# New durations in a kernel's emission-order model, a 128-row up-projection and a weight stream of its own

## The chip, the core and the metric

The kernel runs on one core of one Trainium2 chip. The metric is the device time of one execution in microseconds. The kernel of before took 1872.74 us, the median of three runs (1870.92, 1872.74 and 1876.2).

## What is computed

One step of an encoder layer: RMS norm, one input projection for two groups of heads, a mixer in each group, a SiLU gate, one output projection, and a second norm with a residual. There are T = 1088 tokens: a prompt of 1024 and a sample of 64 that continues a cache of 128. Cut to what matters:

```python
h = _rms_norm(x, norm_pre, NORM_EPS)
proj = h @ w_in                                    # 1024 -> 8320 columns
# group A: 8 heads of differential attention, two softmaxes per head
q, k = _partial_rope(...), _partial_rope(...)
s = jnp.einsum('bqhcd,bkhcd->bchqk', q, k).astype(F32) * (A_QK_DIM ** -0.5)
s = jnp.where(visible[None, None, None], s, -jnp.inf)
p = jax.nn.softmax(s, axis=-1)
wgt = p[:, 0] - lam * p[:, 1]
o = jnp.einsum('bhqk,bkhd->bqhd', wgt.astype(v.dtype), v)
y_a = _rms_norm(o, subln, SUBLN_EPS) * (1.0 - lambda_init) * silu(gate_a)
# group B: 16 heads of RWKV-7 with a 64 x 64 state each
w_log = -softplus(-(w0 + jnp.tanh(wd) @ w_up)) - 0.5        # wd, ad: 64 columns
a = jax.nn.sigmoid(a0 + ad @ a_up)
s = s * w_t + sa * b_t + v_t * k_t                 # per token, sa = s @ a_t
y_b = (group_norm(s @ r_t) + bonus) * silu(gate_b)
out = concat(y_a, y_b) @ w_out                     # 2048 -> 1024
x_new = x + _rms_norm(out, norm_post, NORM_EPS)
```

## The kernel before, in words

**The four kinds of work.** (1) The input projections: `proj_cm` (L208) makes 128 columns of `proj` for all tokens, as three chunks of 384, 384 and 320 tokens; each chunk is 8 times 3 matmuls, since every operand is split into a high and a low half (L215 high x high, L216 high x low, L217 low x high). (2) Group B: `unit` (L476) handles one pair of heads over 512 tokens; there are 16 of them, and one more for the sample that holds all 16 heads (17 in all). A unit takes the up-projection of decay and rate (L513 with the high half of the weights, L514 with the low half), elementwise work, the inverse of a triangular matrix in levels (L684 and L694), and then a serial chain over eight steps of 64 tokens. A step of the chain is three times the same alternation of TensorE (PE) and VectorE (DVE): L804 makes `g` and DVE copies it (L818), L821 makes `uu` and DVE copies it into `suv` (L827 and L828), L832 makes the state's update and DVE adds it (L842). The unit ends with a norm, transposes (L906) and its output to DRAM. Its matmuls L804 to L833 go through one PSUM bank, `cbank`. (3) Group A, `phase_a`: per head `prep` loads and splits queries and keys, `score` makes the scores of a tile of 128 queries (L1322 and L1323), reduces their maximum on DVE (L1332) and takes the exponential on ScalarE (ACT, L1348); `qtile` combines the two softmaxes on DVE (L1370), transposes the weights (L1381), copies them out (L1385 on DVE, L1389 on ACT), multiplies by the values (L1395), and ends with a norm and a gate (L1412 and after). Heads run one after the other. (4) The output projection, `out_projection` (L1041): 72 `jobs`, which are 8 groups of contraction rows and output columns by 9 tiles of tokens. Groups 0 to 3 need only group B's output, groups 4 and 5 the first four heads of A, group 6 heads 4 and 5, group 7 heads 6 and 7. A job is 12 matmuls of 512 columns (L1145, L1146 and L1147) in L1145's loop, and its result is added up in SBUF by ACT or DVE. The weights of a group are loaded by `load_wo` (L1074; 8 DMAs of 256 columns, each followed by a split on ACT and POOL), the tokens' side by `load_mix` (L1090); `loader` (L1108) goes over the jobs and starts both.

**What sets the order.** All instructions are emitted by one scheduler, the class `Weave` (L64). Every piece of work above is a stream (a Python generator) with a rank: the units have 0 to 16 and come first, the projections of group A follow as filling with rank 100, the heads of A have ten ranks each, the output projection fills at rank 99. `Weave` holds a model time `now`. A stream emits some instructions, says what they cost (`spend(ns)` for PE, `op(engine, n)` for an operation of n elements on another engine, which returns the time until its result is there), and yields for so long. At every turn the stream of lowest rank whose time has come goes on; if none is due, model time jumps. So the durations of the model say how much filling is put between a matmul and the one that needs its result by way of DVE or ACT. The framework then places semaphores and moves some instructions within an engine's queue, so the order that results is read from the built program. The lines that set the model are

```python
LA, LAT, W_LD, W_DMA = 130, 100, 11000, 3122                   # L42
...
    def spend(self, ns):
        self.now += ns
    def op(self, eng, n):
        self.free[eng] = max(self.now, self.free.get(eng, 0.0)) + RS * (RATE[eng] * n + 80)
        return self.free[eng] - self.now + (LA if b_done[0] else LAT)
```

DMAs of both `load_wo` and `load_mix` are issued by the queue of SyncE (SP), and so are most of the heads' loads and the outputs.

Of the kernel before, what the change touches and what calls it, by code (L numbers as in the profile page):

```python
# [21 lines left out]
P = 128  # L22
# [19 lines left out]
LA, LAT, W_LD, W_DMA = 130, 100, 11000, 3122  # L42
# [4 lines left out]
RS = 1.0  # L47
RATE = {DVE: 1 / 0.96, ACT: 1 / 1.2, POOL: 2.4}

# [9 lines left out]
class Weave:  # L59
# [7 lines left out]
    def __init__(self):  # L67
        self.now = 0.0
        self.live = []
        self.free = {}  # L70
        self.count = itertools.count()
# [46 lines left out]
def layer(ctx: ExitStack, tc: tile.TileContext, I, O):  # L118
# [105 lines left out]
    def raw_rows(tag):  # L224

        raw = rp.tile([P, T + 1], F32, tag="raw", bufs=2, name=f"raw_{tag}")
        nc.gpsimd.memset(raw[:, 0:1], 0.0)

        def evac(ps, t0, n):
            nc.scalar.copy(raw[:, 1 + t0:1 + t0 + n], ps)  # L230
        return raw, evac
# [50 lines left out]
def phase_b(tc, I, O, E):  # L282
# [8 lines left out]
    with ExitStack() as bs:  # L291
# [68 lines left out]
        def shift(raw, idx, dest):  # L360
# [34 lines left out]
        def pair_job(nm, p, w):  # L395
# [10 lines left out]
            if nm == "g":  # L406
                h0, h1 = yield from tiles()

                def evac(ps, t0, n):
                    for s0, s1, d in ((0, HALF, h0), (HALF, TP, h1), (TP, T, gs_[:, p, :])):  # L410
# [5 lines left out]
                        stt(d_, d_, 1.0, ps[:, a - t0:b - t0], op0=ADD, op1=MUL)  # L416
                yield from proj_cm(w, evac, f"g{p}")
# [58 lines left out]
        def unit(n, p, hf):  # L476
# [21 lines left out]
            for q0 in range(0, 8, 4) if smp else (0,):  # L498
# [43 lines left out]
            spend(1100)  # L542
# [13 lines left out]
            yield op_(DVE, 512)  # L556
# [62 lines left out]
            op_(POOL, 960)  # L619
            op_(ACT, 512)  # L620
# [6 lines left out]
            for g in range(2):  # L627
# [7 lines left out]
                spend(1800)  # L635
# [9 lines left out]
                yield done(op_(DVE, 6 * 256 + 400), 2)  # L645
# [26 lines left out]
            d = op_(DVE, 800)  # L672
# [7 lines left out]
            for lv in range(1, 6):  # L680
# [4 lines left out]
                spend(300)  # L685
# [9 lines left out]
                spend(500)  # L695
# [15 lines left out]
            spend(500)  # L711
# [12 lines left out]
            spend(600)  # L724
# [7 lines left out]
            for h in range(2):  # L732
# [5 lines left out]
                spend(500)  # L738
# [27 lines left out]
            spend(500)  # L766
# [35 lines left out]
            for c in range(8):  # L802
# [41 lines left out]
                op_(DVE, 110)  # L844
                if c % 4 == 3:
# [7 lines left out]
                    op_(ACT, 400)  # L853
                    op_(ACT, 400)
                yield op_(DVE, 110)
# [8 lines left out]
            yield op_(DVE, 1200)  # L864
# [9 lines left out]
            yield op_(POOL, 700)  # L874
# [3 lines left out]
            z_at = weave.now + op_(POOL, 110)  # L878
# [45 lines left out]
            vtt(yo, yo, gate, op=MUL)  # L924
            if smp:
# [6 lines left out]
        def fill_job(kind, h, w):  # L932
# [3 lines left out]
            def evac(ps, t0, n):  # L936
                if kind == "g":
                    act(st_[:, t0:t0 + n], ps, AF.Tanh, scale=0.5)
                    stt(st_[:, t0:t0 + n], st_[:, t0:t0 + n], 1.0, ps, op0=ADD, op1=MUL)  # L939
                else:  # L940

                    act(st_[:, t0:t0 + n], ps, AF.Copy, scale=0.125 if kind == "q" else 1.0)
            yield from proj_cm(w, evac, f"a{kind}{h}")
# [9 lines left out]
        def rope(kd, g):  # L953
            W = T // 8
            for j in range(8):
# [10 lines left out]
                vtt(a, a, b, op=ADD)  # L966
                nc.sync.dma_start(out=E["rots"][kd, g, 2][:, cl], in_=a)
# [72 lines left out]
def out_projection(tc, I, O, E):  # L1040
# [95 lines left out]
    weave.add(99, loader())  # L1136
    for i, (g, tt) in enumerate(jobs):
# [26 lines left out]
def phase_a(tc, I, O, E):  # L1164
# [49 lines left out]
    def prep(h):  # L1214
# [75 lines left out]
        for c in range(2):  # L1290
# [5 lines left out]
            spend(450)  # L1296
# [9 lines left out]
    def score(i, h, qt, c, st):  # L1306
# [12 lines left out]
        for o_, w in parts:  # L1319
# [4 lines left out]
            spend(w / 1.2 + 20)  # L1324
        yield LA
        nb = ap_.tile([P, 3], F32, tag=f"nb{c}", bufs=3, name=f"nb{u}")
        for i_, (s, (o_, w)) in enumerate(zip(ss, parts)):
            if qt < 8 and i_ == m - 1:

                nc.vector.memset(s[0:64, w - 64:w], -(2.0 ** 100))  # L1330
                op_(DVE, 60)
# [3 lines left out]
        if m > 1:  # L1335
            mx = nb[:, 2:3]
            vtt(mx, nb[:, 0:1], nb[:, 1:2], op=ALU.min)  # L1337
            d = op_(DVE, 60)
# [158 lines left out]
```

## Time and profile before

| what | value |
|---|---|
| runs of before | 1876.2, 1870.92, 1872.74 us; median 1872.74 |
| the profiled execution | 1870.95 us, of which the span of its instructions is 1869.1 us |
| granted TensorE clock, mean over the span | 0.975 of full speed |
| PE, busy share of the span | 91% (12,930 matmuls) |
| DVE / ACT / POOL, busy share | 70% / 46% / 37% |
| DMA | 158.85 MB, mean 85 GB/s |

The profile is of one execution. A busy share is a mean over the span; the span has stages with different limits: group B's units come first, then group A's attention with the output projection, then the last jobs and the final norm. An instruction's line is that of the kernel of before; in the kernel of after the same instructions stand 12 to 20 lines further down (L513 and L514 at L526 and L527, L215 to L217 at L224 to L226, L804 at L818, L821 at L835, L832 at L846, L906 at L919, L1145 to L1147 at L1165 to L1167, L1322 and L1323 at L1342 and L1343, L1381 at L1401, L1395 at L1415).

### The profile page before, as it was taken

The page shows a single profiled execution, that of the slowest core. Times are in us where ns is not written, and L with a number is a line of the kernel's source. Part 1 is how long each engine was busy: PE and PEld are TensorE (multiplying, and loading weights), DVE is VectorE, ACT ScalarE, POOL GpSimd, SP SyncE. Part 2 cuts the span into 40 slices and gives each one's busy share as a digit, 9 for nine tenths or more (in the row PEclk, how much of TensorE's full clock was granted, in tenths as well). Part 3 has the DMA queues.
Part 4 walks back from the last instruction along what each step waited for, and adds up shares of the span by engine and source line. Part 5 has one row for each costly group of instructions (what it writes and reads, how often), then busy time and mean ns, then how long its engine had stood idle before and what let it go on. Part 6 is the DMA issues. An engine that isn't in the chain of part 4 may idle for free. (4 is left out here: it accounts for less than half of the span.)

```text
span 1869.1 us, 34871 instructions
## 1 busy us (share of the span) xinstructions
PE 1699.6 (91%) x12930; PEld 1500.6 (80%) x12930; DVE 1305.8 (70%) x2892; ACT 868.1 (46%) x2155; POOL 695.4 (37%) x866
## 2 busy tenths in 40 slices
PE   6999899999998999999999899977899798889995
PEld 5888888888888888888888789877778676777784
DVE  5568777777778787886875766524687667787336
ACT  5534444344344444444443433323566576676323
POOL 4442333233233323323332421212332356554657
PEclk9999999999999999999999999998999899899998
DMA  4110111321122111110101121345555565443325
GB/s 144 49 55 27 50 48 48 80 82 36 39 72 62 51 44 35 52 38 29 57 26 50 57 62 50 106 118 160 153 156 149 165 155 156 121 131 105 116 87 181
DMA packets 204244, 158.85 MB, mean 85 GB/s; under 512 B 44229, under 2 KB 185194, under 8 KB 204074
## 3 DMA queue, kind: packets, MB, share of 16 engines
q1 hardware_dynamic: 169242, 137.33, 25.5%
q10 hardware_dynamic: 34832, 19.30, 4.0%
q8 instruction: 102, 1.67, 0.4%
q14 instruction: 68, 0.56, 0.1%
HBM read 108.67 MB, written 47.34 MB: 83 GB/s over the span
## 5 line engine op out<-in xcount | busy, mean ns | idle before, releaser
L1348 ACT ACTIVATE e<-s,nb 128x512 f32<-128x512 f32 (+4 forms) x208 | 117.3, 569 | 59.3 <-DVE nb L1332 26.1
L1145 PE MATMUL po<-woh,mxh 128*128 128x512 f32 x288 | 120.3, 419 | 7.1 <-DVE part L1156 5.9
L1147 PE MATMUL po<-wol,mxh 128*128 128x512 f32 x288 | 115.9, 402 | 3.9 <-DVE nb L1337 2.5
L1146 PE MATMUL po<-woh,mxl 128*128 128x512 f32 x288 | 115.5, 401 | 4.2 <-POOL mxl L158 4.2
L1332 DVE TENSOR_REDUCE nb<-s 128x1 f32<-128x512 f32 (+4 forms) x208 | 108.0, 529 | 15.9 <-PE s L1323 14.6
L158 POOL TENSOR_TENSOR mxl<-mxr,mxh 128x512 fp32r<-128x512 f32 (+1 forms) x72 | 88.3, 1231 | 74.9 <-ACT mxh L157 61.8
L811 ACT ACTIVATE sd<-suv,dc 64x64 f32<-64x64 f32 x128 | 44.4, 347 | 154.1 <-DVE suv L842 149.4
L1322 PE MATMUL s<-k,qs 128*128 128x512 f32 (+4 forms) x208 | 78.9, 385 | 22.0 <-ACT k L1249 10.0
L1395 PE MATMUL x_o<-vn,wt 128*128 128x128 f32 (+1 forms) x608 | 88.0, 289 | 10.1 <-DVE wt L1385 5.4
L1395 PEld LDWEIGHTS x_o<-vn,wt 128*128 128x128 f32 (+1 forms) x608 | 81.0, 200 | 18.5 <-issue 5.5
L1156 DVE TENSOR_TENSOR part<-po,part 128x512 f32<-128x512 f32 x72 | 49.5, 688 | 55.6 <-PE po L1147 55.5
L842 DVE SCALAR_TENSOR_TENSOR suv<-cbank,dc,sd 64x64 f32<-64x64 f32 x224 | 63.0, 281 | 33.3 <-PE cbank L832 29.2
L832 PE MATMUL cbank<-suv,bkt 128*128 128x128 f32 x256 | 56.9, 304 | 32.0 <-DVE suv L828 32.0
L832 PEld LDWEIGHTS cbank<-suv,bkt 128*128 128x128 f32 x256 | 41.1, 190 | 45.7 <-DVE suv L828 43.4
L215 PE MATMUL pj_v<-hhi,wh_v 128*128 128x384 f32 (+1 forms) x192 | 70.1, 365 | 6.5 <-DVE mg L416 6.1
L1409 POOL TENSOR_SCALAR ms<-ms 128x1 f32<-128x1 f32 x72 | 18.0, 249 | 150.9 <-ACT osq L1407 150.4
L1323 PE MATMUL s<-k,qs 128*128 128x512 f32 (+4 forms) x208 | 71.5, 358 | 2.4 <-POOL k L1252 1.5
L215 PE MATMUL pj_av<-hhi,wh_av 128*128 128x384 f32 (+1 forms) x192 | 70.2, 365 | 3.0 <-DVE fl_g L939 3.0
L157 ACT CAST mxh<-mxr 128x512 fp32r<-128x512 f32 (+1 forms) x72 | 40.7, 567 | 68.7 <-PE po L1147 29.4
L677 POOL TENSOR_TENSOR ltlo<-lt,lt 64x512 f16<-64x512 f32 x32 | 37.7, 1177 | 93.4 <-ACT lt L665 92.2
L1145 PEld LDWEIGHTS po<-woh,mxh 128*128 128x128 f32 x288 | 55.4, 192 | 20.6 <-DVE part L1156 4.4
L215 PE MATMUL pj_k<-hhi,wh_k 128*128 128x384 f32 (+1 forms) x192 | 67.7, 352 | 4.0 <-ACT raw_k L230 4.0
(533 smaller groups left out, 6189.5 us busy)
## 6 DMA issues: line engine op xcount, KB each, us to landing
mxr<-mixB SPq DMA_DIRECT2D x32, 256.0 KB
wor<-in_w_out SPq DMA_DIRECT2D x64, 128.0 KB
qa<-scr_q SPq DMA_DIRECT2D x32, 204.0 KB
ka<-scr_k SPq DMA_DIRECT2D x32, 204.0 KB
scr_q<-fl_q SPq DMA_DIRECT2D x8, 544.0 KB
scr_k<-fl_k SPq DMA_DIRECT2D x8, 544.0 KB
scr_v<-fl_v SPq DMA_DIRECT2D x8, 544.0 KB
scr_g<-fl_g SPq DMA_DIRECT2D x8, 544.0 KB
```

Of the source, the lines that this page charges most:

```text
L158: gtt(lo, raw, hi.bitcast(F32), op=SUB)
L215: mm(ps[:, :n], hi[:, k, :], hhi[i][:, k, :], start=(k == 0), stop=False)
L832: mm(s, bkt[:, c], suv[:, c], start=True, stop=True)
L842: stt(suv[r, c + 1, h, :] if c < 7 and not smp else to[r], s[r, h * CH:(h + 1) * CH], dc[r, c:c + 1], sd[r], op0=MUL, op1=ADD)
L1145: mm(ps, hi[:, q, :], wh, start=(q == 0), stop=False)
L1146: mm(ps, lo[:, q, :], wh, start=False, stop=False)
L1147: mm(ps, hi[:, q, :], wl, start=False, stop=(q == len(ks) - 1))
L1322: mm(s[:, 0:w], lq, k1[c][:, k0 + o_:k0 + o_ + w], start=True, stop=False)
L1323: mm(s[:, 0:w], lq, k2[c][:, k0 + o_:k0 + o_ + w], start=False, stop=True)
L1332: nc.vector.tensor_reduce(nb[:, i_:i_ + 1], s[:, 0:w], axis=AX.X, op=MAX, negate=True)
L1348: act(e[:, o_:o_ + w], s[:, 0:w], AF.Exp, bias=mx, accum_out=sm)
L1395: mm(ops[:, 0:P], wt[0:w, b, :], vn[0:w, vb, :], start=(b == 0), stop=(b == len(kbs) - 1))
```

## The change

Three things change. First, the model's durations: fixed costs per operation (`FIX`), a latency of 210 ns after matmuls and 60 ns after other engines in place of 130 and 100, a cost for switching to and from matmuls that use only part of the 128 rows (`T_IN`, `T_OUT`), new numbers in many calls of `spend` and `op_`, and calls for operations that the model did not have. Second, the low half of the up-projection (L514) multiplies all 128 rows of `t` and `x`, where it took the 64 rows that hold the high half of `x`; so it also adds low x low. Third, the weights of the output projection are loaded by a stream of their own (`w_loader`, rank 99.2), group after group, each as soon as the group before the last is done; before, `loader` started that when it came to a group's first job, behind its waits for the tokens' side. The core of the diff:

```diff
-LA, LAT, W_LD, W_DMA = 130, 100, 11000, 3122
+LAT, OUT, W_LD, W_DMA = 210, 60, 11000, 3122
+LA = LAT
+
+T_IN, T_OUT = 130, 105
...
+FIX = {DVE: 150, ACT: 190, POOL: 90}
...
-    def spend(self, ns):
+    def spend(self, ns, part=False):
+
+        if part != self.part:
+            self.part = part
+            ns += T_IN if part else T_OUT
         self.now += ns
 
-    def op(self, eng, n):
-
-        self.free[eng] = max(self.now, self.free.get(eng, 0.0)) + RS * (RATE[eng] * n + 80)
-        return self.free[eng] - self.now + (LA if b_done[0] else LAT)
+    def op(self, eng, n, k=1, at=0.0):
+
+
+        self.free[eng] = max(self.now + at, self.free.get(eng, 0.0)) + RATE[eng] * n + k * FIX[eng]
+        return self.free[eng] - self.now + OUT
...
                 for q, t in enumerate(ups):
-                    for j, (x, r) in enumerate(((xw, slice(0, 64)), (xa, slice(64, 128)))):
+                    for j, x in enumerate((xw, xa)):
...
                         mm(o_, t[:, j], x[:, cl], start=True, stop=False)
-                        mm(o_, t[r, 2 + j], x[r, cl], start=False, stop=True)
+                        mm(o_, t[:, 2 + j], x[:, cl], start=False, stop=True)
                 spend(900)
...
-                spend(500)
+                spend(340, True)
                 yield LAT
                 xn = t512("xt", 2, F16, nm=f"{lv}{u}")
...
-            spend(w / 1.2 + 20)
+            spend(w / 1.1 + 10)
         yield LA
...
-        op_(ACT, n)
-        return op_(POOL, n)
+        return op_(POOL, n, at=op_(ACT, n))
...
     def loader():
         for q, (g, tt) in enumerate(jobs):
-            if q % 9 == 0:
-                yield lambda: done[0] >= 9 * (g - 1)
-                weave.add(99.2, load_wo(g))
             yield lambda: there(g, tt) and q < done[0] + MB and len(mix) + done[0] >= q - 1
             weave.add(99.1, load_mix(q))
             yield 10
+
+    def w_loader():
+
+        for g in range(8):
+            yield lambda: done[0] >= 9 * (g - 1)
+            yield from load_wo(g)
...
     weave.add(99, loader())
+    weave.add(99.2, w_loader())
```

How this moves instructions on PE is read from the built programs, at three places. In the rows a name ends in a running number of the allocation, and "x2" is a run of two.

**First place: the up-projection of the first unit of head pair 3.** `m_up` is the up-projection, `xw` and `xa` its inputs, `t_wus` the weights, `pj_` a chunk of a projection, `y` and `cbank` belong to the chain of the unit before. Before:

```order
L694 MATMUL m_iq12_10_5076<-xt_a2_1_4974,q16_12_1_5037 64x64
L804 MATMUL cbank_509<-suv2_0_4717,pt0_498 128x128
L809 MATMUL y2_00_4807<-suv2_0_4717,pt0_498 128x128
L513 MATMUL m_up3_00_5068<-xw_466,t_wus3_00_5070 128x512
L514 MATMUL m_up3_00_5068<-xw_466,t_wus3_00_5070 128x512
L513 MATMUL m_up3_01_5069<-xa_467,t_wus3_00_5070 128x512
L514 MATMUL m_up3_01_5069<-xa_467,t_wus3_00_5070 128x512
L215 MATMUL pj_r3_0_5062<-hhi0_173,wh_r3_4843 128x384
```

and of the change:

```order
L225 MATMUL pj_av0_0_5348<-hlo0_176,wh_av0_5092 128x384
L226 MATMUL pj_av0_0_5348<-hhi0_173,wl_av0_5093 128x384
L224 MATMUL pj_av0_0_5348<-hhi0_173,wh_av0_5092 128x384
L225 MATMUL pj_av0_0_5348<-hlo0_176,wh_av0_5092 128x384
L226 MATMUL pj_av0_0_5348<-hhi0_173,wl_av0_5093 128x384
L526 MATMUL m_up3_00_5379<-xw_466,t_wus3_00_5381 128x512
L527 MATMUL m_up3_00_5379<-xw_466,t_wus3_00_5381 128x512
L526 MATMUL m_up3_01_5380<-xa_467,t_wus3_00_5381 128x512
L527 MATMUL m_up3_01_5380<-xa_467,t_wus3_00_5381 128x512
```

The four matmuls stand together in both; the projections around them (`pj_r3`, a chunk of this unit's own inputs, before; `pj_av0`, a chunk of group A's, after) are others.

**Second place: a step of the chain of the last unit, 7_1.** `gsb` and `suv` are what DVE hands over between L821 and L832 (L835 and L846), `po` are the output projection's results. Before:

```order
L215 MATMUL pj_ak5_2_14946<-hhi2_175,wh_ak5_14536 128x320
L216 MATMUL pj_ak5_2_14946<-hlo2_178,wh_ak5_14536 128x320
L217 MATMUL pj_ak5_2_14946<-hhi2_175,wl_ak5_14537 128x320
L821 MATMUL cbank_509<-gsb7_14_14958,xtf_504 128x128
L824 MATMUL y7_14_14954<-suv7_1_14687,pt0_498 128x128
L215 MATMUL pj_ak5_2_14946<-hhi2_175,wh_ak5_14536 128x320
L216 MATMUL pj_ak5_2_14946<-hlo2_178,wh_ak5_14536 128x320
L217 MATMUL pj_ak5_2_14946<-hhi2_175,wl_ak5_14537 128x320
L215 MATMUL pj_ak5_2_14946<-hhi2_175,wh_ak5_14536 128x320
L216 MATMUL pj_ak5_2_14946<-hlo2_178,wh_ak5_14536 128x320
L217 MATMUL pj_ak5_2_14946<-hhi2_175,wl_ak5_14537 128x320
L832 MATMUL cbank_509<-suv7_1_14687,bkt7_1_14656 128x128
```

and of the change:

```order
L1166 MATMUL po000_16272<-woh90_16234,mxl00_16219 128x512
L1167 MATMUL po000_16272<-wol90_16235,mxh00_16218 128x512
L818 MATMUL cbank_509<-suv7_1_15879,pt0_498 128x128
L838 MATMUL y7_14_16034<-suv7_1_15879,pt0_498 128x128
L1165 MATMUL po010_16288<-woh90_16234,mxh01_16224 128x512
L1166 MATMUL po010_16288<-woh90_16234,mxl01_16225 128x512
L835 MATMUL cbank_509<-gsb7_14_16038,xtf_504 128x128
L1165 MATMUL po000_16272<-woh100_16248,mxh00_16218 128x512
L1166 MATMUL po000_16272<-woh100_16248,mxl00_16219 128x512
L1167 MATMUL po000_16272<-wol100_16249,mxh00_16218 128x512
L846 MATMUL cbank_509<-suv7_1_15879,bkt7_1_15848 128x128
L847 MATMUL y7_14_16034<-suv7_1_15879,rbk7_1_15188 128x128
```

Before, projections of head 5 stand between the chain's matmuls, six of them between L824 and L832; after it all projections are used up and the output projection's matmuls stand there, three in that gap.

**Third place: head 3, tile 5.** `s3_5` are scores, `x_wt` transposed weights, `x_o` the product with the values. Before:

```order
L1381 MATMUL x_wt3_20_18161<-ident_79,e3_20_18091 128x128 x2
L1322 MATMUL s3_41512_18154<-k131_17847,qs31_17822 128x128
L1323 MATMUL s3_41512_18154<-k231_17865,qs31_17822 128x128
L1145 MATMUL po000_18238<-woh80_17903,mxh00_17909 128x512
L1395 MATMUL x_o3_8_18184<-vn3_17377,wt3_8_18099 128x128 x2
L1146 MATMUL po000_18238<-woh80_17903,mxl00_17910 128x512
L1322 MATMUL s3_500_18190<-k130_17800,qs30_17760 128x512
L1323 MATMUL s3_500_18190<-k230_17820,qs30_17760 128x512
L1147 MATMUL po000_18238<-wol80_17904,mxh00_17909 128x512
L1145 MATMUL po010_18318<-woh80_17903,mxh01_17915 128x512
L1381 MATMUL x_wt3_30_18200<-ident_79,e3_30_18133 128x128 x4
L1322 MATMUL s3_50512_18193<-k130_17800,qs30_17760 128x256
```

and of the change:

```order
L1343 MATMUL s3_410_19084<-k231_18842,qs31_18797 128x512
L1415 MATMUL x_o3_8_19068<-vn3_18328,wt3_8_19033 128x128 x2
L1342 MATMUL s3_41512_19087<-k131_18817,qs31_18797 128x128
L1343 MATMUL s3_41512_19087<-k231_18842,qs31_18797 128x128
L1401 MATMUL x_wt3_20_19094<-ident_79,e3_20_19039 128x128 x3
L1315 MATMUL x_kt31_19106<-ident_79,ka31_18321 128x64 x8
L1342 MATMUL s3_500_19130<-k130_18763,qs30_18744 128x512
L1343 MATMUL s3_500_19130<-k230_18795,qs30_18744 128x512
L1342 MATMUL s3_50512_19133<-k130_18763,qs30_18744 128x256
L1343 MATMUL s3_50512_19133<-k230_18795,qs30_18744 128x256
L1401 MATMUL x_wt3_30_19136<-ident_79,e3_30_19048 128x128 x4
L1415 MATMUL x_o3_2_19141<-vn3_18328,wt3_2_19093 128x128 x3
```

Before, output-projection matmuls stand one by one between the attention's; after it none is there, and the attention's matmuls follow each other.

## Rows read from the trace of the kernel before

**Rows 1.** The page's part 1: busy time and share of each engine.
```profile
PE 1699.6 (91%) x12930; PEld 1500.6 (80%) x12930; DVE 1305.8 (70%) x2892; ACT 868.1 (46%) x2155; POOL 695.4 (37%) x866
```

**Rows 2.** Stretches: length; busy of PE, PEld, DVE, ACT, POOL; clock, DMA share, GB/s.
```profile
100.00:1240.00 1140.00, 1079.45 (x9432) 973.92 (x9431) 840.02 (x1818) 471.98 (x1076) 352.28 (x419) 0.99 0.18 53
1300.00:1740.00 440.00, 391.92 (x2381) 333.76 (x2380) 326.05 (x842) 280.43 (x843) 197.38 (x254) 0.96 0.53 143
1821.00:1869.00 48.00, 29.18 (x110) 20.50 (x108) 31.83 (x37) 16.87 (x34) 34.65 (x44) 0.89 0.53 179
```

**Rows 3.** Timeline of PE at one up-projection: start us, duration us, instruction.
```profile
1076.23 0.40 PE L513 MATMUL m_up<-xw,t_wus 128*128 128x512 f32 x1
1076.56 0.50 PE L514 MATMUL m_up<-xw,t_wus 64*128 64x512 f32 x1
1076.99 0.50 PE L513 MATMUL m_up<-xa,t_wus 128*128 128x512 f32 x1
1077.42 0.49 PE L514 MATMUL m_up<-xa,t_wus 64*128 64x512 f32 x1
1077.85 0.49 PE L804 MATMUL cbank<-suv,pt 128*128 128x128 f32 x2
```

**Rows 4.** Timeline of PE: output projection, projection in a run, projection after another kind.
```profile
1764.80 0.39 PE L1145 MATMUL po<-woh,mxh 128*128 128x512 f32 x1
1765.03 0.39 PE L1146 MATMUL po<-woh,mxl 128*128 128x512 f32 x1
...
604.56 0.34 PE L215 MATMUL pj_v<-hhi,wh_v 128*128 128x384 f32 x1
604.73 0.34 PE L216 MATMUL pj_v<-hlo,wh_v 128*128 128x384 f32 x1
...
601.92 0.44 PE L215 MATMUL pj_v<-hhi,wh_v 128*128 128x384 f32 x1
602.20 0.34 PE L216 MATMUL pj_v<-hlo,wh_v 128*128 128x384 f32 x1
```

**Rows 5.** Timeline of PE in the sample unit's up-projection (L514 lies between).
```profile
1013.83 0.28 PE L513 MATMUL m_upNone<-xw,t_wusNone 128*128 128x64 f32 x1
...
1014.26 0.30 PE L513 MATMUL m_upNone<-xa,t_wusNone 128*128 128x64 f32 x1
```

**Rows 6.** Instructions of one line: ns min/median/max, first to last start us, forms.
```profile
L906 PE MATMUL m_zt<-ident,ycp x128: 270/272/327, 194.5 to 1233.0; 128*128 128x128 f32 x128
L1322 PE MATMUL s<-k,qs x208: 218/391/795, 1262.7 to 1726.1; 128*128 128x512 f32 x72, 128*128 128x128 f32 x8, 128*128 128x256 f32 x8, 128*128 128x192 f32 x8
L1395 PE MATMUL x_o<-vn,wt x608: 270/275/582, 1275.8 to 1738.7; 128*128 128x128 f32 x151, 64*128 64x128 f32 x1
```

**Rows 7.** PE's waits, 100 to 1240 us: total us, times, longest us.
```profile
PE cbank L832 <- DVE suv L828: 32.0, 36, 3.2
PE cbank L821 <- DVE gsb L818: 7.7, 9, 1.8
```

**Rows 8.** Tile cbank in the last unit, 1196 to 1223 us (two records a matmul).
```profile
L832 PE MATMUL cbank<-suv,bkt x14: 271/275/377, 1196.2 to 1222.5; 128*128 128x128 f32 x14
```

**Rows 9.** Stretches of the attention, columns as in rows 2.
```profile
1341.00:1682.50 341.50, 302.86 (x1840) 256.27 (x1840) 258.29 (x664) 225.96 (x671) 158.48 (x197) 0.97 0.55 148
...
1460.60:1471.40 10.80, 8.03 (x51) 5.76 (x49) 10.01 (x39) 6.02 (x22) 0.74 (x2) 1.00 0.67 200
1471.40:1477.00 5.60, 0.40 (x2) 0.20 (x2) 0.14 (x1) 1.72 (x5) 1.03 (x1) 0.58 0.93 318
1253.80:1274.30 20.50, 6.98 (x27) 5.86 (x27) 6.68 (x21) 8.28 (x18) 5.54 (x3) 0.50 0.77 198
...
1541.00:1552.00 11.00, 8.99 (x53) 6.69 (x52) 10.21 (x26) 8.05 (x28) 1.18 (x3) 1.00 0.62 175
```

**Rows 10.** Groups by line on DVE, 1341 to 1682.5 us.
```profile
L1332 DVE TENSOR_REDUCE nb<-s 128x1 f32<-128x512 f32 (+4 forms) x156 | 81.1, 529 | 13.3 <-PE s L1323 12.3
```

**Rows 11.** ACT's waits for mix loads, 1440 to 1740 us.
```profile
ACT mxh L157 <- DMA mxr<-mixB: 10.9, 4, 5.7
```

More of the change, by code (lines that the diff above doesn't have):

```diff
@@ L230, in evac @@
             nc.scalar.copy(raw[:, 1 + t0:1 + t0 + n], ps)
+            weave.op(ACT, n, at=LAT)
         return raw, evac
@@ L367, in shift @@
                 act(d, raw[:, t0 + 1:t0 + 1 + n], AF.Copy, scale=omu[:, idx:idx + 1])
+                op_(DVE, n, at=op_(ACT, n + 80))
                 if t0 == TP:
@@ L416, in evac @@
                         stt(d_, d_, 1.0, ps[:, a - t0:b - t0], op0=ADD, op1=MUL)
+                        op_(DVE, b - a, at=op_(ACT, b - a, at=LAT))
                 yield from proj_cm(w, evac, f"g{p}")
@@ L555, in unit @@
             nc.gpsimd.memset(dd[:, :, 0:1], 1.0)
-            yield op_(DVE, 512)
+            yield op_(DVE, 1020)
             act(dd[:, :, 1:CH + 1], c3(cs), AF.Exp, scale=-C2)
@@ L605, in unit @@
             vtt(kb, kb, rm, op=MUL)
-            op_(DVE, 512)
+            op_(POOL, 512)
             free.add(("r", p, hf))
-            op_(DVE, 4100)
+            op_(DVE, 8 * 512, 8)
             kbh = t512(dt=F32R, nm=f"kbh{u}")
@@ L618, in unit @@
                 stt(kbl, kb, hrk[:, p:p + 1], kbh.bitcast(F32), op0=MUL, op1=SUB)
-            op_(POOL, 960)
-            op_(ACT, 512)
+            if smp:
+                op_(POOL, 512)
+            op_(ACT, 600)
             yield op_(DVE, 512)
@@ L644, in unit @@
                 vtt(rbk[:, gs, 1, :], po3[:, :, CH:], bch(incl, 4), op=MUL)
-                yield done(op_(DVE, 6 * 256 + 400), 2)
+                yield done(op_(DVE, 6 * 256, 6), 2)
             soon.add(("v", p, hf))
@@ L671, in unit @@
             vtt(c3(xt), c3(xt), bch(id16), op=ADD)
-            d = op_(DVE, 800)
+            d = op_(DVE, 1400, 3)
             yield d
@@ L843, in unit @@
                         dc[r, c:c + 1], sd[r], op0=MUL, op1=ADD)
-                op_(DVE, 110)
+                op_(DVE, 128)
                 if c % 4 == 3:
@@ L852, in unit @@
                         nc.scalar.copy(ysb[64:128, 0:CH], y4[64:128, 3, CH:])
-                    op_(ACT, 400)
-                    op_(ACT, 400)
-                yield op_(DVE, 110)
+                    op_(ACT, 570, 3)
+                yield op_(DVE, 128)
             yield lambda: turn["norm"] == n
@@ L863, in unit @@
             vtt(c3(yc), y3, bcol(mu), op=ADD)
-            yield op_(DVE, 1200)
+            yield op_(DVE, 1040, 3)
             ysq = t512("ysq", 1, nm=u)
@@ L924, in unit @@
             vtt(yo, yo, gate, op=MUL)
+            op_(DVE, 600)
             if smp:
@@ L939, in evac @@
                     stt(st_[:, t0:t0 + n], st_[:, t0:t0 + n], 1.0, ps, op0=ADD, op1=MUL)
+                    op_(DVE, n, at=op_(ACT, n, at=LAT))
                 else:
                     act(st_[:, t0:t0 + n], ps, AF.Copy, scale=0.125 if kind == "q" else 1.0)
+                    op_(ACT, n, at=LAT)
             yield from proj_cm(w, evac, f"a{kind}{h}")
@@ L966, in rope @@
                 vtt(a, a, b, op=ADD)
+                op_(DVE, 3 * W, 3)
                 nc.sync.dma_start(out=E["rots"][kd, g, 2][:, cl], in_=a)
@@ L1337, in score @@
             vtt(mx, nb[:, 0:1], nb[:, 1:2], op=ALU.min)
-            d = op_(DVE, 60)
+            d = op_(DVE, 10)
         yield d
@@ L1370, in qtile @@
         stt(w_[:, 0:n], e1[:, 0:n], co, w_[:, 0:n], op0=MUL, op1=ADD)
-        op_(DVE, 400)
-        yield op_(DVE, n)
+        op_(DVE, 130, 2)
+        yield op_(DVE, n + 60)
         yield lambda: (h, 2) in ready
@@ L1407, in qtile @@
         act(sq, on, AF.Square, accum_out=ms)
-        yield op_(ACT, P)
+        yield op_(ACT, P, 2)
         gts(ms, ms, 1.0 / P, SUBLN_EPS, op0=MUL, op1=ADD)
```

30 lines of the change are left out of this document (15 added, 15 removed).

## The prediction, made before the changed kernel ran

> **What bounds the kernel now.** I read the page's first part, then the table of stretches, then TensorE's (PE's) waits, then timelines. PE is busy 1699.6 of 1869.1 us [rows 1]; the profiled execution took 1870.95 us, 1.85 us around its span, and lies 0.1% under the median of the runs, 1872.74. "Faster" and "slower" mean by over 0.3% of that median, 5.6 us, about what a measurement of this kernel can tell from no change. The stretches [rows 2] tell three regimes. In group B's units (100 to 1240 us) PE is busy 95%, VectorE (DVE) 74%: PE bounds, with small holes. While attention runs (1300 to 1740) PE falls to 89% with DVE at 74%: neither is full. In the last 48 us PE has 29 us of work. So a matmul saved among the units is time saved, while in attention what counts is whether PE has something to fill with.
>
> **Change 1: the low half of the up-projection over 128 rows.** Before, L513 and L514 alternate between 128 and 64 rows. Starts in one unit [rows 3]: 1076.23, 1076.56, 1076.99, 1077.42, and 1077.85 for what follows, 1.62 us for four matmuls of 512 columns. Output-projection matmuls of 512 columns that all use 128 rows start 0.227 us apart [rows 4], so four would take 0.91. Saved: 0.71 us in each of 16 units, 11 us. In the sample unit an L513/L514 pair of 64 columns takes 0.43 us [rows 5]; the nearest row for two small 128-row matmuls is a projection's 0.17 us each at 384 columns [rows 4], and they are smaller, so I take 0.2 per pair: 16 pairs x 0.23 = 4 us. Sum 15 us, all on PE where it is 95% busy, so I take all of it. Bounds: 0 (another wait takes the place) to 20. [...]
>
> **Change 2: the durations in the model.** They move work, they do not remove it. The order shows three moves on PE.
>
> (a) Projections are emitted in longer runs: the count of times that PE comes to a projection from something else falls from 679 to 586 (counted over both orders). Such an entry costs: after another kind L216 starts 0.28 us behind L215, in a run 0.17 [rows 4]. 93 x 0.11 = 10 us less PE time; bounds 0 and 15.
>
> (b) Every unit now takes more filling, so group B ends later with less left over. The order counts, after the last L906, 612 projection matmuls before the change and none after it; 59 output-projection matmuls now stand ahead of that point. At 0.164 us for a projection matmul (0.17 for 384 columns, scaled for the 320 of the third chunk: an estimate) and 0.227, that is +100 and +13 us on 1233.0, where the last L906 starts [rows 6]. PE's waits in the chain: 32.0 us at L832 and 7.7 at L821 [rows 7]. More PE work now stands between producer and consumer at L832 and for most inverse steps, less at L821 and around the last two units. I take 12 us off; bounds 0 and 30. Against it, the last unit's eight chain steps have just 59 x 0.227 + about 7 = 20 us of PE work around them, 2.5 us a step, where the same chain took 26.3 us for six steps, from the first L832 to the seventh, 4.4 each [rows 8]. Between 0 and 15, I take 8. Group B's end: 1233 + 100 + 13 - 15 - 10 - 12 + 8 = 1317. From there to the first score it was 29.7 us [rows 6], with 108 projection matmuls (18 us) as cover; now 73 of the output projection (17 us). The same 29.7: first score at 1347.
>
> (c) Attention: from the first score to the last L1395 it was 476 us [rows 6], with 504 projection and 402 output-projection matmuls between, and stretches longer than 6 us without either held some 33 us of PE work. Now 624 output-projection matmuls stand there, and they run out: all of group B's are used up when head 3 begins, and later groups wait for their heads. Head 0, head 3 with the start of head 4, head 6 and the end of head 7 stand bare: by their score columns 4.6 of 8 heads, about 130 us of PE work. A head costs DVE 258.29 / 6 = 43.0 us, since the 156 reductions of 1341 to 1682.5 are those of six heads [rows 9, 10]. Bare, DVE sets the pace: in the two short bare stretches of before it is busy 10.01 of 10.80 and 10.21 of 11.00 us, 93% [rows 9]. If all of 4.6 heads' DVE work fell inside, they would take 4.6 x 43.0 / 0.93 = 213 us; at PE's own pace 130. The last steps of a tile (L1370, L1385, L1412) fall behind its scores, often into filled stretches, so I take 190. The filled rest: 624 x 0.227 = 142 plus 3.4 heads at 25 (an estimate: 608 L1395 in pieces of 0.11 and the other matmuls of attention by their starts) = 227 us of PE work. 1341 to 1682.5 held 280 x 0.164 + 324 x 0.227 + 6 x 25 = 270 us of it in 341.5, a share of 0.79; one stall of PE, 5.6 us with the loads at 318 GB/s, lies in that [rows 9]. With less DVE work around I take 0.86: 264 us; bounds 0.79 (287) and 0.95 (239). Attention: 190 + 264 = 454, ending at 1801.
>
> After it only the last group is left, 108 matmuls, the same that began at 1821 and took 48 us to the end [rows 2]; 3 us more for the last head's way through DRAM: 1852.
>
> **Change 3: the weights' own stream.** The same 64 loads; a group's weights are asked for as soon as the group before the last is done. On SP the first 18 now stand before group B's last outputs and head 0's loads, which stand behind two mix loads that wait for buffers. ACT waited 10.9 us for mix loads while attention ran, once 5.7 [rows 11]. I cost it at 0, from -6 (that stall goes) to +8.
>
> **Sum.** Span 1852 + 1.85 = **1854 us**, 0.9% under the profiled execution, 1.0% under the median.
>
> **Rivals.**
> *A, the chain's waits mostly go* (change 2b at its best): a wait is then always shorter than the matmuls put before it. For: L832's waits are 36 of up to 3.2 us [rows 7], and the gap there grew. [...] Another 20 us: 1834.
> *B, no change:* the four matmuls and the entries cost as before (0 for 15 + 10), since something else of the step is late. 1854 + 25 = 1879 less what a freer DVE gives back in filled stretches (share 0.88 for 0.86, 6 us): 1873. [...] Against: [rows 3] shows no releaser, just later starts.
> *C, slower: the bare heads.* No fill in heads 0, 3, 6, 7; PE, DVE and ACT wait for each other in turn. DVE there at 84.5%, halfway between 93% and the 76% (258.29 of 341.50) of the filled stretch [rows 9], gives 4.6 x 43.0 / 0.845 = 234 us, 44 more than I took: 1898. It decides from 208 us on, 18 more than I took. For: the 213 above is already past that. Against: the bare stretches of before run at 93%. [...]
>
> **Chances.** Forecast 0.42, A 0.13, B 0.15, C 0.30. Faster 0.55, same 0.15, slower 0.30. Range: A's 1834 widened by the bounds of (b) and of the filled share to 1822; at the top C's 1898: 1822 to 1898. The forecast's own range is 1838 to 1867.
>
> **What would show it.** The four starts at L526/L527 0.23 us apart. The last unit's transposes at 1317 +- 12. Attention 454 us long, with stretches of some 20 us without projections in which DVE is over 90% busy. If DVE is under 85% there, or the clock at 0.50, C holds. L846's waits above 32 us would break (b); four starts still 0.4 apart would break change 1.

## The result, and the profile after

The changed kernel takes 1948.03 us (median of four runs, 1947.22 to 1952.25) against 1874.38, by then the median of four runs of before: a ratio of 1.040, 95% interval 1.0377 to 1.0423. It is slower by 4%, outside the predicted range of 1822 to 1898. The same work fills TensorE (PE) less, as the page's first part shows beside [rows 1]:

```profile
PE 1731.6 (89%) x12930; PEld 1541.7 (79%) x12930; DVE 1314.5 (68%) x2892; ACT 865.9 (44%) x2155; POOL 691.2 (36%) x866
```

**Where it went.** The three marks of [rows 6], in the same view of the changed kernel (ns min/median/max, first to last start):

```profile
L919 PE MATMUL m_zt<-ident,ycp x128: 270/273/476, 214.5 to 1390.7; 128*128 128x128 f32 x128
L1342 PE MATMUL s<-k,qs x208: 218/392/793, 1418.5 to 1887.0; 128*128 128x512 f32 x72, 128*128 128x128 f32 x8, 128*128 128x256 f32 x8, 128*128 128x192 f32 x8
L1415 PE MATMUL x_o<-vn,wt x608: 270/275/580, 1431.3 to 1894.9; 128*128 128x128 f32 x151, 64*128 64x128 f32 x1
```

Group B ends at 1390.7 in place of 1233.0 (+157.7), the way to the first score is 27.8 in place of 29.7, attention takes 476.4 in place of 476.0, and 51.6 us follow to the span's end where 130.4 did (-78.8). Sum +77.4, the whole difference of the spans (1946.5 against 1869.1). The moved matmuls explain 113 of the 157.7 and all of the -78.8 (354 output-projection matmuls at 0.227 are 80 us). So **45 us were lost in group B**, and attention, with 32 us less filling (504 x 0.164 + 402 x 0.227 = 174 us before, 624 x 0.227 = 142 now), **gave nothing back**.

**What TensorE waits for in group B.** Its waits from 100 to 1391 us (total us, times, longest), beside [rows 7]:

```profile
PE cbank L846 <- DVE suv L842: 15.1, 20, 1.8
PE cbank L835 <- DVE gsb L832: 14.4, 13, 2.4
PE m_zt L919 <- ACT suv L769: 13.4, 7, 2.4
PE m_zt L919 <- DVE ycp L888: 10.3, 4, 4.9
PE m_ip L698 <- DVE x L717: 8.8, 6, 3.2
PE m_iq L708 <- DVE q L702: 7.0, 8, 2.1
PE m_zt L919 <- DVE t_kbl L631: 4.2, 1, 4.2
```

The chain waits less than before, as was forecast. New are the norm's transposes (L919; L906 had waited 2.3 us in all, now 30.8) and the inverse (L698 and L708; 4.4 us before, 17.6 now).

**One such wait, looked at closely.** Three timelines of the changed kernel around 816 us (start us, duration us, instruction, and in brackets the idle time before it with its releaser). ScalarE:

```profile
811.40 0.37 ACT L767 COPY suv<-m_vt 64x256 f32<-64x256 f32 x1 [0.57 <-PE m_vt L761]
811.78 0.31 ACT L769 COPY suv<-m_vt 64x192 f32<-64x192 f32 x1
815.94 0.72 ACT L630 ACTIVATE t_kbh<-t_kb,dv 128x512 fp32r<-128x512 f32 x1 [3.85 <-DVE t_kb L618]
816.68 0.37 ACT L767 COPY suv<-m_vt 64x256 f32<-64x256 f32 x1
817.06 0.47 ACT L769 COPY suv<-m_vt 64x256 f32<-64x256 f32 x2
```

VectorE, on which L630 waits:

```profile
813.35 0.69 DVE L616 TENSOR_TENSOR bk<-t_kb,t_cs 64x512 f32<-64x512 f32 x1
815.21 0.69 DVE L618 TENSOR_TENSOR t_kb<-t_kb,mr 128x512 f32<-128x512 f32 x1 [1.18 <-POOL bk L615]
```

TensorE:

```profile
814.47 0.31 PE L225 MATMUL pj_v<-hlo,wh_v 128*128 128x320 f32 x1
814.62 0.31 PE L226 MATMUL pj_v<-hhi,wl_v 128*128 128x320 f32 x1
814.77 0.60 PE L919 MATMUL m_zt<-ident,ycp 128*128 128x128 f32 x4
815.20 0.39 PE L818 MATMUL cbank<-suv,pt 128*128 128x128 f32 x2
817.48 0.65 PE L919 MATMUL m_zt<-ident,ycp 128*128 128x128 f32 x4 [1.89 <-ACT suv L769]
817.89 0.47 PE L224 MATMUL pj_v<-hhi,wh_v 128*128 128x320 f32 x1
818.16 0.47 PE L225 MATMUL pj_v<-hlo,wh_v 128*128 128x320 f32 x1
818.43 0.47 PE L226 MATMUL pj_v<-hhi,wl_v 128*128 128x320 f32 x1
```

ACT's queue has an instruction of the next unit (L630) ahead of three copies (one of L767, two of L769) that free PSUM banks. L630 waits 3.85 us for DVE, and DVE for POOL; so the copies, whose input PE wrote by 813, run at 816.68, and the second half of L919's transposes, which need a bank, at 817.48. Behind them stand projections that wait for nothing. By the built program L630 stands ahead of such copies in 10 of 16 units, L617 before in 1.

**And the clock.** After the wait the projections start 0.27 us apart, where they had started 0.15 apart. The stretches before, at and after it, from which the granted clock (third number from the end) is read:

```profile
809.00:815.00 6.00, 6.00 (x57) 5.29 (x57) 2.67 (x4) 1.99 (x5) 4.00 (x4) 1.00 0.01 3
815.00:817.50 2.50, 0.61 (x7) 0.42 (x5) 1.47 (x3) 1.53 (x5) 0.36 (x3) 1.00 0.00 0
818.10:821.50 3.40, 3.40 (x15) 3.40 (x14) 1.79 (x4) 3.36 (x7) 0.74 (x1) 0.50 0.00 0
```

From 100 us to group B's end the stretches at half clock, added up from the trace, are 95.6 us where they were 17.1. The 1.89 us wait was followed by 3.40 us at a clock of 0.50, but one of 2.41 us at the same line, ending at 365.8 us, was followed by 6 us at 1.00.

### The profile page after: what moved, and what is told of

It is laid out like the page before. It is cut to its first block, busy times and chain, and to the rows that moved or that the text cites. A ratio compares the mean times of both kernels' runs of the same rounds, so it can differ in the third digit from the quotient of the medians.

```text
span 1946.5 us, 34817 instructions
## 1 busy us (share of the span) xinstructions
PE 1731.6 (89%) x12930; PEld 1541.7 (79%) x12930; DVE 1314.5 (68%) x2892; ACT 865.9 (44%) x2155; POOL 691.2 (36%) x866
## 4 chain that ended last, share of the span: by engine, by line
PE 57%; DVE 17%; POOL 8%; DMA 6%; ACT 6%; issue 5%; ACTq 1%; SPq 0%; POOLq 0%; DVEq 0%
PE x_o L1415 3%; PE po L1166 2%; PE po L1165 2%; PE po L1167 2%; PE cbank L846 2%; PE cbank L835 2%; PE pj_av L224 2%; PE pj_ak L224 1%; PE cbank L818 1%; PE pj_aq L224 1%; PE pj_av L225 1%; PE pj_av L226 1%; PE pj_ak L225 1%; PE pj_k L224 1%; PE pj_ak L226 1%
## 5 line engine op out<-in xcount | busy, mean ns | idle before, releaser
L1165 PE MATMUL po<-woh,mxh 128*128 128x512 f32 x288 | 126.1, 439 | 25.1 <-DVE part L1176 17.6
L1415 PE MATMUL x_o<-vn,wt 128*128 128x128 f32 (+1 forms) x608 | 94.3, 302 | 5.0 <-ACT kt L1318 1.7
L1415 PEld LDWEIGHTS x_o<-vn,wt 128*128 128x128 f32 (+1 forms) x608 | 86.1, 211 | 15.5 <-ACT wt L1405 3.8
L856 DVE SCALAR_TENSOR_TENSOR suv<-cbank,dc,sd 64x64 f32<-64x64 f32 x224 | 63.0, 281 | 37.8 <-PE cbank L846 33.3
L702 DVE TENSOR_TENSOR q<-m_ip,mt 128x512 f16<-128x512 f32 x80 | 55.1, 689 | 31.3 <-PE m_ip L698 30.4
L1342 PEld LDWEIGHTS s<-k,qs 128*128 128x128 f32 x208 | 41.4, 201 | 40.6 <-ACT e L1368 29.1
L846 PE MATMUL cbank<-suv,bkt 128*128 128x128 f32 x256 | 58.7, 312 | 15.2 <-DVE suv L842 15.1
L1166 PEld LDWEIGHTS po<-woh,mxl 128*128 128x128 f32 x288 | 57.3, 199 | 17.6 <-POOL mxl L167 9.5
L224 PE MATMUL pj_g<-hhi,wh_g 128*128 128x384 f32 (+1 forms) x192 | 70.5, 367 | 0.0
```

Of the source, the lines that this page charges most:

```text
L224: mm(ps[:, :n], hi[:, k, :], hhi[i][:, k, :], start=(k == 0), stop=False)
L846: mm(s, bkt[:, c], suv[:, c], start=True, stop=True)
L856: stt(suv[r, c + 1, h, :] if c < 7 and not smp else to[r], s[r, h * CH:(h + 1) * CH], dc[r, c:c + 1], sd[r], op0=MUL, op1=ADD)
L1165: mm(ps, hi[:, q, :], wh, start=(q == 0), stop=False)
L1166: mm(ps, lo[:, q, :], wh, start=False, stop=False)
L1342: mm(s[:, 0:w], lq, k1[c][:, k0 + o_:k0 + o_ + w], start=True, stop=False)
```

## The experiments

The table holds all runs; each ratio is against the kernel of before on the same chip. "B ends" is the last start of the norm's transposes, "attention" goes from the first score to the last product with the values, "half" is the time at half clock from 100 us to B's end; these three come from one profile each.

| kernel | median us | ratio (95%) | B ends | attention | half |
|---|---|---|---|---|---|
| before | 1874.38 | 1 | 1233.0 | 476.0 | 17.1 |
| changed | 1948.03 | 1.040 (1.0377 to 1.0423) | 1390.7 | 476.4 | 95.6 |
| e1_up128 | 1869.06 | 0.998 (0.9964 to 0.9998) | 1227.6 | 479.7 | 20.5 |
| e2_wstream | 1869.32 | 0.999 (0.9972 to 1.0001) | 1228.8 | 496.8 | 20.5 |
| e0_both | 1865.35 | 0.995 (0.9939 to 0.9969) | 1227.7 | 499.2 | 20.5 |
| x1_const | 1887.99 | 1.008 (1.0057 to 1.0106) | 1303.1 | 490.6 | 51.2 |
| x2_calls | 1897.86 | 1.013 (1.0112 to 1.0146) | 1311.0 | 455.1 | 44.4 |
| e3_model | 1936.03 | 1.035 (1.0312 to 1.0381) | 1397.0 | 456.7 | 85.3 |
| e5_kbhdve | 1937.33 | 1.035 (1.0322 to 1.037) | 1376.7 | 481.2 | 86.5 |
| e4_ztlate | 1916.06 | 1.023 (1.0214 to 1.0245) | 1360.0 | 476.9 | 61.4 |
| e6_nostream | 1925.24 | 1.027 (1.0223 to 1.0308) | 1383.8 | 456.5 | 78.5 |
| e7_comb | 1912.57 | 1.020 (1.0171 to 1.0236) | 1380.1 | 458.3 | 85.3 |
| e9_zt_nostream | 1891.43 | 1.010 (1.007 to 1.0122) | 1356.8 | 458.2 | 54.6 |
| e10_morelate | 1921.15 | 1.026 (1.0237 to 1.0276) | 1377.5 | 454.7 | 95.0 |
| e8_chain300 | 1857.15 | 0.990 (0.987 to 0.9934) | 1251.5 | 474.3 | 27.3 |

### Each part alone

**e1_up128**: before, and

```diff
-                    for j, (x, r) in enumerate(((xw, slice(0, 64)), (xa, slice(64, 128)))):
+                    for j, x in enumerate((xw, xa)):
...
-                        mm(o_, t[r, 2 + j], x[r, cl], start=False, stop=True)
+                        mm(o_, t[:, 2 + j], x[:, cl], start=False, stop=True)
```

> The kernel of before with only the 128-row low half of the up-projection; order of everything else unchanged. Theory M (the emission model's new durations make TensorE wait for other engines, and its clock falls after the waits): the row change is worth what its starts say, 0.7 us in each of 16 units plus about 4 us in the sample unit, so 11 to 15 us less than before: about 1860. Rival U (something else of the step is late, so the rows save nothing): 1874, and the next wait of the step grows by what the four matmuls lost.

1869.06, 0.2% less. Between the two expectations: group B ends 5.4 us earlier, and attention is 3.7 us longer with the same order. In B the chain took most of the rest, about 8 us; its longest waits in the kernel with the 128 rows (100 to 1240 us), where [rows 7] have 32.0 and 7.7:

```profile
PE cbank L832 <- DVE suv L828: 36.4, 36, 3.2
PE cbank L821 <- DVE gsb L818: 10.9, 13, 1.8
```

So PE, 95% busy over these 1140 us before, was not yet the bound: with less to do, it waited more for DVE, 47.3 us at these two lines where it had been 39.7.

**e2_wstream**: before, and `w_loader` as in the change.

> The kernel of before with only the weights' own stream. By its order 96 output-projection matmuls move from behind the last attention matmul into attention (498 there instead of 402). Theory M: they fill attention, so up to 96 x 0.227 = 22 us less: 1852 to 1874. Rival W (the stream is what costs in the change, since weight loads stand ahead of the heads' loads in SyncE's queue and hold up attention): slower than before by 10 us or more, 1885 or above.

1869.32, which can't be told from no change. Rival W falls; the 22 us of filling that moved into attention made attention 21 us longer (496.8).

**e3_model**: the change without its other two parts (the loader's old lines come back as shown at e6_nostream),

```diff
-                        mm(o_, t[:, 2 + j], x[:, cl], start=False, stop=True)
+                        mm(o_, t[r, 2 + j], x[r, cl], start=False, stop=True)
...
-    weave.add(99.2, w_loader())
```

> The kernel of before with only the new durations in the model (64-row up-projection, weights started by the loader). Theory M: the whole loss is here: 1948 plus the 11 to 15 us of the row change = 1955 to 1965, with waits of TensorE at the norm's transposes of some 35 us up to the end of group B, as in the changed kernel. Rival W: clearly under 1948, since the stream is gone.

1936.03: the durations alone cost 3.5%. But it is under 1948, not over it by the rows' worth, and the two profiles differ in attention: 456.7 here, 476.4 in the changed kernel. So with the new order one of the other parts costs time. That led to:

**e6_nostream**: the changed kernel with the weights started by the loader.

```diff
         for q, (g, tt) in enumerate(jobs):
+            if q % 9 == 0:
+                yield lambda: done[0] >= 9 * (g - 1)
+                weave.add(99.2, load_wo(g))
...
-    weave.add(99.2, w_loader())
```

> The changed kernel with the weights again started by the loader; the 128-row up-projection and the new durations stay. Theory S (with the new order the stream costs time in attention, since it makes the first groups' matmuls come in head 1 in one lump of 204 and leaves heads 3, 6 and 7 bare): group B ends near 1391 as before, attention takes about 457 us as in the kernel with the durations alone, and the time is about 1929. Rival R (the 128-row matmuls cost those 20 us, by moving the order): attention stays at 476 and the time near 1948.

1925.24, attention 456.5: it is the stream. By the trace the 624 output-projection matmuls stand in heads 0 to 7 as 0, 204, 96, 0, 117, 99, 60, 48 in the changed kernel, and as 0, 123, 87, 92, 106, 84, 102, 30 here; stretches of over 6 us without one add up to 218 us there and 151 here. Attention in both (length, then PE's busy time, its count of matmuls and further on the clock, third number from the end), the changed kernel first:

```profile
1418.50:1894.90 476.40, 404.08 (x2248) 330.81 (x2249) 349.89 (x888) 282.91 (x857) 209.82 (x272) 0.92 0.44 120
...
1412.10:1868.50 456.40, 393.18 (x2248) 320.00 (x2249) 346.94 (x888) 281.63 (x857) 210.18 (x274) 0.94 0.46 125
```

With the same matmuls PE is busy 11 us longer at a lower clock, and idle 9 us longer. That the lump is the cause, and not the loads themselves, is argued and not shown: no wait of PE's matmuls there is put down to a DMA, and those of all engines together are 23 us in the changed kernel and 19 here. Against e3_model the 128 rows are worth 11 us by the medians (B ends 13 us earlier).

**e0_both**: before with the rows and the stream, and the old durations.

> The kernel of before with the 128-row up-projection and the weights' own stream, and the old durations. Alone, the two gave 0.19% and 0.13% less (1869.06 and 1869.32 against 1872.97). If they add: about 1867. If theory M holds (only the new durations cost), it is at or under before; if the stream costs as it seems to in the changed kernel's attention (476 us there, 457 without it), it is 1880 or more.

1865.35: the two add up, and the kernel beats before by 0.46%.

### Which of the durations

**x1_const**: before with only the general constants.

```diff
-LA, LAT, W_LD, W_DMA = 130, 100, 11000, 3122
+LAT, OUT, W_LD, W_DMA = 210, 60, 11000, 3122
...
+        self.free[eng] = max(self.now + at, self.free.get(eng, 0.0)) + RATE[eng] * n + k * FIX[eng]
+        return self.free[eng] - self.now + OUT
```

> The kernel of before with only the model's general constants (latency 210 and 60, fixed cost per operation), the numbers at the calls as before; 64-row up-projection, weights started by the loader. By its order 4314 projection matmuls stand ahead of the last norm transposes (4068 before, 4680 in the changed kernel), and on ScalarE L617 stands ahead of the copies of the transposed values in 2 of 16 units (1 before, 10 in the changed kernel). Theory M (queue order inside group B makes TensorE wait, and the clock falls): under 1885, since few of these inversions are there. Rival F (each filling matmul that leaves attention for group B costs its share of the 63 us): 246 of 671 moved, 37%, so about 1896.

**x2_calls**: the rest, with the old constants, `k` fixed costs of 80 per call and no price for switching rows.

> The kernel of before with only the numbers at the calls (and the calls added for operations that the model lacked), the general constants as before. By its order 4416 projection matmuls stand ahead of the last norm transposes, and L617's inversion on ScalarE is there in 7 of 16 units. Theory M: 1900 to 1920, with waits at the norm's transposes of 15 us or more. Rival F: 348 of 671 moved, 52%, so about 1906; the two differ here in the waits, not the time: F wants no more waits in group B than before.

1887.99 and 1897.86. Each set costs something alone, 0.8% and 1.3%; together they cost 3.5%, more than the sum. The first time lies between what M and F said, the second under both. M's sign of the loss, the inversions on ACT, was too narrow: x1_const has the inversion in 2 units only, and its norm transposes still wait, 13.8 us on L884 (the same `ycp`); x2_calls waits there for 5.4 us in all, not 15. F wanted no more waits in group B than before, and PE's idle time from 100 us to B's end is 72.9 us in x2_calls against 60.6 before. These two don't settle it; the next does.

**e4_ztlate**: the changed kernel, with one number.

```diff
-            z_at = weave.now + op_(POOL, 220)
+            z_at = weave.now + op_(POOL, 220) + 2500
```

> The changed kernel with one number: the norm's transposes are held back 2.5 us longer in model time, so that filling stands where TensorE waited. Theory M: of the 35 us of waits at L919 most go, with some of the 96 us at half clock after them: 1915 to 1930. Rival F: 1945 to 1955, for the filling that stands there is missing elsewhere.

1916.06, 32 us less by one number, with the same counts of filling in attention and behind it (624 and 108). That refutes F as an account of these 32 us: not where the filling went cost them, but what stands between a matmul and what it waits for. TensorE's waits (100 to 1360 us):

```profile
PE cbank L846 <- DVE suv L842: 28.1, 26, 3.8
PE cbank L835 <- DVE gsb L832: 16.2, 14, 1.9
PE m_zt L919 <- DVE ycp L888: 10.4, 3, 4.8
PE m_iq L708 <- DVE q L702: 6.6, 10, 1.4
```

L919's wait on L769 is gone, and 34 us of half clock with it; 15 us of waits came back in the chain. By ACT's order in the trace L630 still stands ahead of such copies in 9 of 16 units, so the inversion costs time only where PE has no other work until the copies are done.

**e5_kbhdve**: the changed kernel, with L630 on DVE.

```diff
-                act(kbh, kb, AF.Copy, scale=hrk[:, p:p + 1])
+                vts(kbh, kb, hrk[:, p:p + 1], None, op0=MUL)
+                op_(DVE, 512)
...
-            op_(ACT, 600)
+                op_(ACT, 600)
```

> The changed kernel with one operation moved: the high half of the bonus product (L630, ScalarE, 16 of 0.7 us) is computed on VectorE instead, so ScalarE's queue no longer waits there for VectorE and GpSimd ahead of the copies that free the PSUM bank of the transposed values. Theory M: the late copies are what TensorE waits for at the second half of the norm's transposes (13 us at L919 put down to L769), so those waits go, the half-clock stretches after them go too (96 us of half clock up to the end of group B fall to under 70), and the time is 1915 to 1935. Rival A (the loss is attention without filling; group B's waits only stand in for each other): 1945 to 1955, since VectorE has 11 us more work.

1937.33, 11 us less. The model is told of the move too (the last two edits), so PE's order shifts a little: 67 output-projection matmuls stand ahead of B's end in place of 59. What PE and its weight loads waited for at the transposes (total us, times), in the changed kernel and then here:

```profile
  ACT suv L769: 33.3, 16
  DVE ycp L888: 15.6, 6
  issue: 9.7, 4
```

```profile
  DVE ycp L889: 23.6, 8
  issue: 17.9, 6
  ACT suv L770: 0.6, 2
```

The late copies are shown to be the cause of that wait: with the instruction out of ACT's queue it falls from 33.3 to 0.6. But the half clock stayed at 86.5, not under 70, and other waits grew, here those on `ycp` and L835's from 14.4 to 20.1.

**e7_comb**: e4, e5 and e6 together. **e9_zt_nostream**: e4 and e6 together.

> The changed kernel with three edits together: the norm's transposes 2.5 us later in model time, the high half of the bonus product on VectorE, the weights started by the loader. Alone the first two gave 32 and 11 us; the third should give 19. If they are independent: 1948 - 62 = 1886. If the second is a part of the first (both take the same waits at L919 away): about 1895. Under 1873 would say that nothing is left of the loss; theory M expects it to stay over that, for the waits in the inverse (28 us against 11 before) and the bare heads remain.

> The kernel of the combination without its VectorE edit: the changed kernel with the norm's transposes 2.5 us later in model time and the weights started by the loader. If the two are independent (32 and 23 us alone): 1948 - 55 = 1893, with the chain's waits back near 59 us from the 65 of the combination; then the VectorE edit cost 20 us there by making the chain wait. If the delay's 32 us hung on the stream's order: 1910 or more, as in the combination.

1912.57 and 1891.43. e7 missed both of its forecasts, 1886 and 1895, by 18 us and more. e9 says why: the delay and the stream are independent (1893 expected). The 16 operations of 0.7 us on DVE, which gave 11 us in the changed kernel, cost 21 here: L835's waits (lines as in the changed kernel) are 19.1 instead of 16.1, L708's 9.5 instead of 6.3, L698's 8.9 instead of 4.0, and half clock is 85.3 instead of 54.6. The wait that the edit took away was already covered; the load on DVE stayed. e9 is as far as the loss was taken back: 55 of the 74 us. It is still 1% over before, with 27.4 us of waits at L846 and 54.6 us of half clock in group B; what these last 19 us are was not tried.

### The lesson, tried

**e8_chain300**: e0_both, and the chain's wait between L828 and L832 300 ns longer in the model.

```diff
-                yield op_(DVE, 64)
+                yield op_(DVE, 64) + 300
```

> Not the change but its lesson: the kernel of before with the 128 rows and the stream (1865.35), and one number, 300 ns more in the model for the chain's wait between L828 and L832, where TensorE waited 32 us in all. By its order 147 projection matmuls more stand ahead of the last norm transposes. If a number that is raised only where the trace shows the wait takes that wait away (36 waits, 32 us) and nothing else moves: 1845 to 1858. If the filling is missed in attention as much as it helps: 1860 to 1868. If the moved order makes new waits, as the change did: over 1870.

1857.15, the best kernel of all, 1% under before (0.987 to 0.9934). The time is as expected, the way there is not. TensorE's waits from 100 to 1252 us:

```profile
PE cbank L832 <- DVE suv L828: 16.2, 15, 3.8
PE cbank L821 <- DVE gsb L818: 14.2, 13, 2.7
PE cbank L804 <- DVE suv L842: 10.4, 14, 1.5
PE m_zt L906 <- DVE ycp L875: 6.1, 7, 2.0
```

L832's wait is halved, but L821, L804 and L906 took it over (PE's idle time from 100 us to B's end is 74.0 us, 67.8 in e0_both): group B ends 24 us later than in e0_both, just the 147 more projections x 0.164. The gain stands in attention and behind it (599.0 us from B's end to the span's end, 638.6 in e0_both, and only 24 of these 40 are moved work). These are one profiled execution each, which lie 16 us apart where the medians lie 8. Which row of attention the gain comes from stays open.

**e10_morelate**: e9_zt_nostream with the same 300 ns.

> The same with 300 ns more for the chain's wait between L842 and L846, as in the best kernel so far. There 4068 projection matmuls had been placed up to group B's end, and others were left to fill with. Here all 4680 are used up before that end by either kernel. Theory M with a limited stock of filling: the waits only move to the last units, which get nothing more, and the time stays within 10 us of the kernel without the 300 ns. Rival: waits go wherever the model is made later, and it gains 15 us or more, as in the best kernel (8 to 10 us there with 36 waits).

1921.15, 30 us more: neither expectation. L846's wait hardly moves (25.2 us, 27.4 without the 300 ns), L708's goes from 6.3 to 14.2, and L919's from 10.4 to 15.1. The number that gained in one order loses in another.

## Why the prediction was wrong

The sign was wrong, and the step that failed is **(b), "Group B's end: 1233 + 100 + 13 - 15 - 10 - 12 + 8 = 1317"**; it came at 1390.7, 74 us later, because PE waited and ran slow where the sum has no term for it. Term by term:

- *The moved work, +113*: right. The trace has the 59 output-projection matmuls ahead of that point and no projection behind it.
- *The 128 rows, -15*: nearly right as PE time. The four starts are 0.23 us apart, as called for:

```profile
66.90 0.40 PE L526 MATMUL m_up<-xw,t_wus 128*128 128x512 f32 x1
67.14 0.39 PE L527 MATMUL m_up<-xw,t_wus 128*128 128x512 f32 x1
67.37 0.39 PE L526 MATMUL m_up<-xa,t_wus 128*128 128x512 f32 x1
67.59 0.39 PE L527 MATMUL m_up<-xa,t_wus 128*128 128x512 f32 x1
```

  In the new order the 128 rows were worth 13 us of group B (e6 against e3), in the old one 5 (e1). "I take all of it" was the error there.
- *Entries into projections, -10*: mis-sized. The 93 were counted over the whole program; from 100 us to group B's end the traces have 581 before and 558 now, 23 x 0.11 = 2.5 us. Of the others 69 lay behind group B's end, where no projection is left.
- *The chain's waits, -12*: right. L832, L821 and L804 (now L846, L835 and L818) waited 41.9 us and wait 33.2. The last unit's +8 is in that: its chain waited 2.4 us and waits 5.5.
- *Missing: waits where there had been none.* Norm transposes +28.5, inverse +13.2. The order was read for how much stands between the chain's matmuls, not for what stands ahead of the copies on ACT, though ACT's order shows L630's inversion as plainly. That inversion is 13.4 us of the 30.8 at the transposes; 12.0 are waits on `ycp` (L888), whose cause no run looked for. PE's idle time from 100 us to that point went from 60.6 to 93.1 us, about these two and the chain's -8.7.
- *Missing: the clock.* 78.5 us more of half clock. By the distance of each start from the usual one of its pair, about 27 us (22 to 34, by how a slow start is counted) are matmuls that ran slower, above those of before; the rest is waiting, counted above, or time that the same work takes at full speed. The prediction asked after the clock in attention only.

The sum 113 - 13 - 2.5 - 8.7 + 28.5 + 13.2 + 27 is 157.5; measured: 157.7. So close a fit is luck, given the range of the last term.

**(c), attention, 454**: 476.4. The stretches over 6 us without filling, put at 190, are 218; the filled rest, put at 264, is 258. DVE's share in the long bare ones (third busy number, in order of time; PE's is the first):

```profile
1418.50:1466.60 48.10, 30.09 (x148) 23.12 (x148) 33.35 (x97) 27.08 (x81) 14.32 (x18) 0.72 0.51 122
...
1592.80:1662.90 70.10, 51.05 (x301) 42.32 (x299) 58.45 (x144) 45.68 (x137) 29.79 (x38) 0.85 0.45 115
...
1803.00:1832.70 29.70, 25.59 (x158) 20.03 (x157) 26.25 (x88) 21.11 (x74) 5.49 (x13) 0.94 0.51 132
...
1854.40:1894.90 40.50, 34.69 (x236) 28.19 (x235) 32.81 (x105) 26.78 (x93) 7.40 (x20) 0.98 0.22 62
```

150.9 of 188.4 us, 80%, not 93%: the two rows of 11 us that stood for it [rows 9] were pieces of an attention that was otherwise filled. Rival C called this and the sign, at 84.5%, but priced it at 44 us in attention; 28 came, and the larger loss lay in group B, which no rival named. The clock, whose 0.50 was the other sign named for C, was granted at 0.72 to 0.98 on the mean of each of these stretches. **Change 3**, costed at 0 from -6 to +8, costs about 20 us in this order and nothing in the old one. They are most of the 22 by which attention is over its 454: without the stream it takes 456.5.

## What to carry to other kernels

When a change moves instructions, go through the queue of every engine that PE waits for, not PE's alone: an instruction of the next piece of work ahead of a copy that frees a bank can be a new wait (33.3 us here, 0.6 with L630 out of ACT's queue), and a wait can be followed by a stretch at half clock (3.4 us after the one of 1.89 us, on a PE that was 93% busy from 100 to 1391 us). A truer model of durations need not give a better order; numbers that were tuned together carry waits that the model doesn't know, so change one, look at which wait it moved, and keep it only with a measured time. And a saving on the busiest engine is a saving only until the engine that it waits for is as late: the 128 rows were put at 15 us, and in e1 group B ended 5.4 us earlier.

## What was not expected of the hardware

A single wait of 1.89 us after a stretch in which PE had been busy for 6.00 of 6.00 us was followed by 3.4 us at a clock of 0.50, and one of 2.41 us at the same line by none. In all the changed kernel runs at half clock for 95.6 us in group B and 80.2 us in attention; before it was 17.1 and 42.6.
